# Layer 0, second token group: memory attention beside the output gate, its output parked in the recurrence's key tiles

## The chip, the cores and the metric

The kernel runs on one core of a Trainium2 chip. The metric is the device time of one execution in microseconds (us). Before the change the median of three runs is 2419.86 us (2419.42 to 2420.16).

## What is computed

One inference step of a two-layer decoder. 1024 prompt tokens (one sequence) and 8 sample tokens (one each of 8 sequences) share all weights. Layer 0's mixer, cut to what matters here:

```python
def a_mixer(hn, w_in, lb, hg_gain, mem_k, mem_v, w_o, s0):
    q_h, f_h, i_h, g_h, q_m = jnp.split(hn @ w_in, 5, axis=-1)
    ...
    o, S = hgrn2_scan(q, k, v, logf, s0)
    o = rmsnorm(o.astype(hn.dtype), hg_gain) * jax.nn.silu(g_h).reshape(B, L, HG_HEADS, HG_DV)
    om = mem_attend(q_m.reshape(B, L, MEM_HEADS, MEM_DH), mem_k, mem_v)
    out = jnp.concatenate([o.reshape(B, L, MIX_HALF), om.reshape(B, L, MIX_HALF)], axis=-1) @ w_o
    return out, S

def mem_attend(q, mk, mv):
    s = jnp.einsum('blhd,bmhd->bhlm', q.astype(jnp.float32), mk.astype(jnp.float32)) * (q.shape[-1] ** -0.5)
    p = jax.nn.softmax(s, axis=-1)
    return jnp.einsum('bhlm,bmhd->blhd', p, mv.astype(jnp.float32)).astype(q.dtype)
```

There are 4 heads of 128, and 256 memory tokens. The prompt tokens attend to one memory, projected inside the kernel; each sample token attends to a cached memory of its own and carries a recurrence state of its own, 4 heads of 128 x 128, which is read, updated and written back. A SwiGLU feed-forward network (FFN) follows each mixer; layer 1's mixer is another kind of attention.

## The kernel before

The tokens are held in two groups with features on the partitions: group 0 has 512 prompt tokens, group 1 has 512 prompt tokens and the 8 sample tokens. Every float32 product of a projection is split into a high and a low part and takes three matmuls. A projection's matmuls all come from the helper at L222, 24 of 128 x 512 or (group 1) 48 of 128 x 260 for 128 output features and 1024 input features; the weights are loaded by SyncE (L203) and split by ScalarE (L208) and VectorE (L209). Activations are split in the same way by L229 (ScalarE) and L230 (VectorE).

The code is made of Python generators. `weave` (L178) takes generators with a rate each and advances the one that has made the least progress for its rate; this sets the order in which instructions are written. A scheduler then orders them on each engine. Every engine, SyncE's transfers included, executes in that order and waits in it.

Around the change there are two weaves, called here stage A and stage B:

- **Stage A** (L1729) weaves group 1's sample recurrence (`a1.sample`), its output gate (`a1.gate`, L247 to L251: a clamp, three activations and a product), a part of group 0's FFN (`f0.part(1)`) and sums of weights on the DMA queues (`w0`).
- **Stage B** weaves first the product of gate and recurrence (`a1.merge`), then the prompt tokens' memory attention (`a1.mem`), and beside them the sample tokens' memory attention (`a1.mem_sample`) and the rest of group 0's FFN.

The prompt tokens' memory attention (`mem_attn`, L967) loads the memory's keys and values (L970, L971) into two tiles, and then goes through 8 steps, two for each head: scores (L1010), maximum (L1015), exponentials with their sums (L1021), reciprocal and scaling (L1025, L1027), transposes (L978) with a copy out of PSUM (L983) one step later, and the values (L991) two steps later. After two steps a head is complete and `put` splits it into the input tiles `xo` of the output projection (L229, L230).

The sample recurrence (`hgrn_sample`, L1222) transposes the values (L1225), writes them to DRAM (`vd`, L1229) and reads them back broadcast to all partitions. For each head it loads the state and the broadcast values (L1240, 512 KB each) one head ahead, multiplies both (L1253, L1254), adds (L1255), stores the new state (L1256), multiplies by the queries (L1257), splits the result (L229, L230) and sums it by four matmuls (L1262). After the last head the result goes through DRAM (`od`, L1270 and L1272) to be transposed (L1275).

The sample tokens' memory attention (`sample_scores`, L1037, and what follows it) writes the queries to DRAM (`qd`, L1049) and reads one broadcast per token into a tile of pool B (L1055), loads the token's keys (L1099), multiplies and reduces (L1057, L1058); the scores of all 8 tokens are then transposed (L1125).

Pools that matter: C has 4 tiles of 512 KB, for the states, the broadcast `vd`, the memory's keys and values and the cached keys and values alike. B has 7 tiles of 256 KB, T has 3 (the gate's and the FFN's intermediates), A has 8 (the recurrence's forget gates F, keys K and queries Q, two each, and the memory queries `Qm`; the gate's result `sg` takes the next that comes free). In PSUM, `S` has 3 single banks, `NS` one, and `mm` two pairs, which the projections of L222 use in turn; a pair is free when VectorE (L247, L819, L414) has read it.

Of the kernel before, what the change touches and what calls it, by code (L numbers as in the profile page):

```python
# [23 lines left out]
def tile_decoder(  # L24
# [6 lines left out]
    nc = tc.nc  # L31
# [4 lines left out]
    H = 4  # L36
# [4 lines left out]
    G = 512  # L41
# [56 lines left out]
    def NS():  # L98
        return nsp.tile([P, 512], F32, tag="ns", name=nm("ns"))
# [21 lines left out]
    def S():  # L121
        return smp.tile([P, 512], F32, tag="s", name=nm("s"))
# [51 lines left out]
    def chain(*gens):  # L174
        for g_ in gens:
            yield from g_

    def weave(*streams):  # L178

        live = [[0, n, g_] for g_, n in streams]  # L180
        while live:
            cur = min(live, key=lambda e: e[0] / e[1])
            cur[0] += 1
            try:
                next(cur[2])
            except StopIteration:
                live.remove(cur)
# [44 lines left out]
    def put(xo, i, cols, src):  # L232
        if isinstance(xo, list):
            split_to((xo[i][:, 0, cols], xo[i][:, 1, cols]), src)
            return
        t = B()[:, : cols.stop - cols.start]
        nc.scalar.copy(t, src)
        nc.sync.dma_start(xo[:, i, cols], t)
# [725 lines left out]
        yield  # L964


    def mem_attn(g, l, qm, xo):  # L967
        mkt, mv = C(), C()
        mk = mkt.rearrange("p a (h n) -> p (a h) n", n=NM)
        nc.sync.dma_start(mk, mks[l])  # L970
        nc.sync.dma_start(mv, mvs[l])  # L971
        po, asked, turned = None, None, None

        def turn(pe):
            pt = S()
            for mb in range(2):
                for j in range(2):
                    nc.tensor.transpose(  # L978
                        pt[:, (mb * 2 + j) * P : (mb * 2 + j + 1) * P],
                        pe[:, j * NM + mb * P : j * NM + (mb + 1) * P], ident,  # L980
                    )
            pts = B()
            nc.scalar.copy(pts[:, :512], pt)  # L983
            return pts

        def values(h, pr, pts):
            nonlocal po
            if pr == 0:
                po = S()
            for mb in range(2):  # L990
                nc.tensor.matmul(  # L991
                    po[:, pr * 256 : (pr + 1) * 256], mv[:, mb, h * P : (h + 1) * P],
                    pts[:, mb * 256 : (mb + 1) * 256], start=(mb == 0), stop=(mb == 1),
                )
            if pr:
                put(xo, H + h, slice(0, G), po)

        def step(new=None):
            nonlocal asked, turned
            old, turned = turned, asked and (*asked[:2], turn(asked[2]))  # L1000
            asked = new
            if old:
                values(*old)

        for h in range(H):
            for pr in range(2):
                ps = S()
                for j in range(2):
                    t0 = (2 * pr + j) * P
                    nc.tensor.matmul(  # L1010
                        ps[:, j * NM : (j + 1) * NM], qm[h // 2][:, h % 2, t0 : t0 + P], mk[:, h, :],
                        start=True, stop=True,
                    )
                nmx = small([P, 2], tag="nmx")
                nc.vector.tensor_reduce(  # L1015
                    nmx, ps.rearrange("p (j n) -> p j n", j=2), axis=AX.X, op=ALU.max, negate=True
                )
                sm = small([P, 2], tag="sme")
                pe = B()
                for j in range(2):  # L1020
                    nc.scalar.activation(  # L1021
                        pe[:, j * NM : (j + 1) * NM], ps[:, j * NM : (j + 1) * NM], AF.Exp,
                        bias=nmx[:, j : j + 1], accum_out=sm[:, j : j + 1],
                    )
                nc.vector.reciprocal(sm, sm)  # L1025
                for j in range(2):
                    nc.vector.tensor_scalar(  # L1027
                        pe[:, j * NM : (j + 1) * NM], pe[:, j * NM : (j + 1) * NM], sm[:, j : j + 1], None,
                        op0=ALU.mult,
                    )  # L1030
                step((h, pr, pe))
                yield
        for _ in range(2):
            step()
            yield
# [186 lines left out]
    def hgrn_sample(Ft, Kt, Qt, vs):  # L1222
        pvv = S()
        for h in range(H):
            nc.tensor.transpose(pvv[:NB, h * P : (h + 1) * P], vs[:, h, :], ident)  # L1225
        vT = B()
        nc.vector.tensor_copy(vT[:NB, :512], pvv[:NB, :])
        vd = tc.dram_tile([NB, 512], F32, name=nm("vd"))
        nc.sync.dma_start(vd, vT[:NB, :])  # L1229
        yield  # L1230
        HB = H * NB
        assert 2 * H == NB

        def fetch(h):
            st, vb = C(), C()
            for t, src in (
                (st, state_hgrn[0, :, h].rearrange("b k v -> k b v")),
                (vb, vd[:, h * P : (h + 1) * P].partition_broadcast(P)),
            ):
                nc.sync.dma_start(t.rearrange("p a (b v) -> p (a b) v", v=P), src)  # L1240
            return st, vb

        nxt = fetch(0)
        yield
        po = S()
        for h in range(H):
            def col(t):
                return t[h // 2][:, h % 2, G : G + NB].unsqueeze(2).to_broadcast([P, NB, P])

            st, vb = nxt  # L1250
            nxt = h < H - 1 and fetch(h + 1)
            stv, vbv = (t.rearrange("p a (b v) -> p (a b) v", v=P) for t in (st, vb))
            nc.vector.tensor_mul(stv, stv, col(Ft))  # L1253
            nc.vector.tensor_mul(vbv, vbv, col(Kt))  # L1254
            nc.vector.tensor_add(st, st, vb)  # L1255
            nc.sync.dma_start(st_sample[0, :, h].rearrange("b k v -> k b v"), stv)  # L1256
            nc.vector.tensor_mul(vbv, stv, col(Qt))  # L1257
            for a in range(2):
                qs = B(F32R), B(F32R)
                split_to(qs, vb[:, a, :])  # L1260
                for i, p in enumerate(qs):
                    nc.tensor.matmul(  # L1262
                        po[:NB, :], selr[:, 2 * h + a, :], p,
                        start=(h == 0 and a == 0 and i == 0), stop=(h == H - 1 and a == 1 and i == 1),
                    )
            yield
        rows = B()
        nc.vector.tensor_copy(rows[:NB, :], po[:NB, :])
        od = tc.dram_tile([H, NB, P], F32, name=nm("od"))
        nc.sync.dma_start(od.rearrange("h (a b) v -> (h a) b v", a=2), rows[:NB, :].rearrange("p (b v) -> p b v", v=P))  # L1270
        ot = B()
        nc.sync.dma_start(ot[:NB, :].rearrange("p (h v) -> p h v", v=P), od.rearrange("h b v -> b h v"))  # L1272
        pr = S()
        for h in range(H):
            nc.tensor.transpose(pr[:, h * NB : (h + 1) * NB], ot[:NB, h * P : (h + 1) * P], ident[:NB, :NB])  # L1275
        oc = small([P, HB], tag="ss")
        nc.scalar.copy(oc, pr[:, :HB])
        osq = small([P, HB], tag="ss")
        nc.scalar.activation(osq, oc, AF.Square)
        r = rstd_from(osq, HB, 1.0 / P, small([P, HB], tag="ss"), S)  # L1280
        for h in range(H):
            nc.vector.scalar_tensor_tensor(
                Ft[h // 2][:, h % 2, G : G + NB], oc[:, h * NB : (h + 1) * NB], hgn, r[:, h * NB : (h + 1) * NB],
                op0=ALU.mult, op1=ALU.mult,
            )
        yield
# [99 lines left out]
    class mixer_a:  # L1386
# [37 lines left out]
                yield  # L1424

        def mem(self):
            yield from mem_attn(self.g, 0, self.Qm, self.xo)

        def mem_sample(self):
            yield from mem_attn_sample(0, self.Qm, self.xo)  # L1430
# [156 lines left out]
    class mixer_b:  # L1587
# [25 lines left out]
            yield from sb_prompt(self.g, self.Qs, self.xo)  # L1613

        def mem(self):
            yield from mem_attn(self.g, 1, self.Qm, self.xo)

        def sb_sample(self):
            yield from sb_sample(self.Qs, self.xo)
# [99 lines left out]
    a1 = mixer_a(1, x1)  # L1719
    weave((chain(a0.gate(), a0.merge()), 8), (start(1, x1), 14))  # L1720
    w0 = weight_sums(0, (3, 4, 2))
# [3 lines left out]
    weave((o0.finish(), 17), (chain(a1.v(), a1.qm(A)), 8), (islice(w0, 12), 13))  # L1725
    f0 = ffn(0, 0, o0.x)
    weave((a1.core(), 22), (f0.part(0), 9), (islice(w0, 16), 17))
    a1.open()
    weave((a1.sample(), 6), (a1.gate(), 4), (f0.part(1), 9), (w0, 9))  # L1729

    def rest():
        yield from f0.part(2)
        set_banks(True)
        fw = ffn_w(0, 0, o0.x, (5, 6, 5), 3, False, f0.R)
        yield from fw.part(3)
        yield from fw.part(4)
        f0.acc = fw.acc

    weave((chain(a1.merge(), a1.mem()), 30), (a1.mem_sample(), 50), (rest(), 24))
    xk0, xb0 = [], []  # L1740
    o1 = out_proj(1, 0, M)
    drain(o1.mm(a1.xo, 0, 1, True))
# [29 lines left out]
    f0 = ffn(0, 1, o0.x)  # L1772
# [51 lines left out]
```

## Time and profile before

| | |
|---|---|
| median of 3 runs | 2419.86 us |
| the profiled execution: time, span, mean granted clock | 2420.19 us, 2418.5 us, 0.997 |
| TensorE (PE) | 99% busy |
| VectorE (DVE) | 72% busy |
| ScalarE (ACT) | 53% busy |
| GpSimd (POOL) | 5% busy |
| DMA, mean over the span | 148 GB/s |

TensorE is busy nearly always, and it executes in program order. What is read from the profile is therefore its few waits: where they are, which engine ended them, and what that engine had waited for. The views used are the busy shares of the page, the list of waits, a table of stretches of 20 us (busy time of each engine, granted clock of TensorE, DMA share), and the timeline of single engines. In the timeline a row has its start, its duration, engine, line, operation, output and inputs, the count of instructions taken together, and in brackets the idle time before it with the engine that ended it. A group's duration runs to the end of its last instruction; from start to start of two rows is what the first one cost.

### The profile page before, as it was taken

How to read it: one execution, taken by the hardware profiler on the slowest of the kernel's cores; microseconds unless marked ns; L12 is line 12 of the kernel's file. 1: busy time of each engine (PE TensorE's matmuls, PEld its weight loads, DVE VectorE, ACT ScalarE, POOL GpSimd, SP SyncE). 2: the span in 40 equal slices, each digit the busy share in tenths (PEclk: the TensorE clock that was granted, in tenths of full speed). 3: DMA queues.
4: the chain of work that ended last, by engine and by line, in shares of the span. 5: the costliest groups of instructions: out<-in, count | busy, mean ns of one | idle time of the engine just before them, and what ended most of it. 6: DMA issues, size and time to landing. Idle time of an engine off the chain costs nothing. (4 is left out here: it accounts for less than half of the span.)

```text
span 2418.5 us, 42360 instructions
## 1 busy us (share of the span) xinstructions
PE 2385.4 (99%) x15959; PEld 2158.9 (89%) x15959; DVE 1732.6 (72%) x3218; ACT 1285.2 (53%) x2560; POOL 118.5 (5%) x187
## 2 busy tenths in 40 slices
PE   8999999999999999999999999999999999999998
PEld 6888988887779998899999989877778899999998
DVE  5867557665787676878566776788788678766866
ACT  5547544354445554666544554555554457554445
POOL 1000201110000000000002200021000000000000
PEclk9999999999999999999999999999999999999999
DMA  6454666577645446432568846455353353343342
GB/s 188 123 166 117 170 189 158 133 182 191 192 132 146 152 136 207 138 101 85 148 173 232 234 138 189 153 165 148 105 165 120 97 162 122 118 129 100 107 130 76
DMA packets 510991, 357.59 MB, mean 148 GB/s; under 512 B 20109, under 2 KB 459514, under 8 KB 510786
## 3 DMA queue, kind: packets, MB, share of 16 engines
q1 hardware_dynamic: 494914, 312.93, 43.4%
q0 software_dynamic: 15872, 41.95, 7.4%
q8 instruction: 126, 2.06, 0.3%
q14 instruction: 79, 0.65, 0.1%
HBM read 322.86 MB, written 65.49 MB: 161 GB/s over the span
## 5 line engine op out<-in xcount | busy, mean ns | idle before, releaser
L222 PE MATMUL mm<-x,ws 128*128 128x512 f32 (+1 forms) x5016 | 924.5, 342 | 5.3 <-DVE t L247 2.9
L222 PEld LDWEIGHTS mm<-x,ws 128*128 128x128 f32 x5016 | 776.6, 188 | 116.9 <-issue 3.7
L208 ACT CAST ws<-w 128x512 fp32r<-128x512 f32 x596 | 347.9, 585 | 433.1 <-PE mm L222 258.9
L209 DVE TENSOR_TENSOR ws<-w,ws 128x512 fp32r<-128x512 f32 x596 | 380.8, 644 | 223.7 <-ACT ws L208 218.8
L751 PE MATMUL q<-m,ws 128*128 128x260 f32 (+1 forms) x2496 | 306.3, 283 | 1.0 <-DVE ws L209 0.4
L751 PEld LDWEIGHTS q<-m,ws 128*128 128x128 f32 x2496 | 300.3, 188 | 3.4 <-ACT m L229 0.8
L578 PE MATMUL q<-y,ws 128*128 128x260 f32 (+1 forms) x1920 | 250.9, 284 | 1.5 <-ACT q L586 1.0
L578 PEld LDWEIGHTS q<-y,ws 128*128 128x128 f32 x1920 | 238.2, 188 | 3.7 <-ACT q L586 1.4
L578 PE MATMUL q<-x,ws 128*128 128x260 f32 (+1 forms) x1668 | 218.6, 283 | 0.2 <-DVE ws L573 0.2
L578 PEld LDWEIGHTS q<-x,ws 128*128 128x128 f32 x1668 | 207.4, 188 | 0.5 <-DVE ws L573 0.4
L222 PE MATMUL mm<-m,ws 128*128 128x512 f32 x768 | 194.1, 403 | 0.2 <-DVE r L414 0.2
L571 ACT CAST ws<-w 128x512 fp32r<-128x512 f32 x206 | 124.7, 618 | 98.0 <-PE q L751 33.0
L573 DVE TENSOR_TENSOR ws<-w,ws 128x512 fp32r<-128x512 f32 x206 | 139.2, 688 | 48.9 <-ACT ws L571 45.0
L222 PEld LDWEIGHTS mm<-m,ws 128*128 128x128 f32 x768 | 143.4, 190 | 32.0 <-DVE r L414 0.7
L760 DVE TENSOR_TENSOR r<-r,q 128x260 f32<-128x260 f32 (+1 forms) x160 | 60.7, 420 | 50.9 <-PE q L751 50.6
L504 PE MATMUL q<-x,ws 128*128 128x260 f32 (+1 forms) x720 | 89.7, 283 | 0.0
L504 PEld LDWEIGHTS q<-x,ws 128*128 128x128 f32 x720 | 87.5, 188 | 0.6
L571 ACT CAST ws<-b 128x512 fp32r<-128x512 f32 x82 | 50.5, 620 | 43.6 <-PE q L751 13.8
L229 ACT CAST m<-t 128x512 fp32r<-128x512 f32 (+1 forms) x88 | 54.8, 623 | 31.0 <-DVE t L619 13.2
L573 DVE TENSOR_TENSOR ws<-b,ws 128x512 fp32r<-128x512 f32 x82 | 56.2, 688 | 18.4 <-ACT ws L571 17.8
L230 DVE TENSOR_TENSOR m<-t,m 128x512 fp32r<-128x512 f32 (+1 forms) x88 | 60.6, 689 | 11.0 <-ACT m L229 10.2
L277 DVE TENSOR_TENSOR st<-st,n 128x512 f32<-128x512 f32 (+1 forms) x91 | 62.1, 690 | 3.6 <-ACT n L276 2.5
(411 smaller groups left out, 3094.4 us busy)
## 6 DMA issues: line engine op xcount, KB each, us to landing
w<-in_w_gu SPq DMA_DIRECT2D x275, 256.0 KB, 3.3
w<-in_w_down SPq DMA_DIRECT2D x160, 256.0 KB, 2.9
wsum<-in_w_gu POOLq DMA_DIRECT2D x48, 512.0 KB, 6.0
w<-in_w_in_a SPq DMA_DIRECT2D x80, 256.0 KB, 3.0
w<-in_w_o SPq DMA_DIRECT2D x64, 256.0 KB, 2.8
w<-wsum SPq DMA_DIRECT2D x61, 256.0 KB, 3.5
b<-in_w_gu SPq DMA_DIRECT2D x39, 256.0 KB, 3.3
b<-wsum SPq DMA_DIRECT2D x39, 256.0 KB, 4.0
```

The lines of the kernel that those rows point to most:

```text
L208: nc.scalar.copy(ws[:, 0, :n, :], raw[:, :n, :])
L209: split[0] = nc.vector.tensor_sub(ws[:, 1, :n, :], raw[:, :n, :], ws[:, 0, :n, :].bitcast(F32))
L222: nc.tensor.matmul(ps[:, a, : PW[g]], wt, xt[k][:, xi, o : o + PW[g]], start=(k == 0 and wi == 0), stop=(k == nk - 1 and wi == 2),)
L229: nc.scalar.copy(dst[0], src)
L230: nc.vector.tensor_sub(dst[1], src, dst[0].bitcast(F32))
L277: nc.vector.tensor_add(acc[:, :n], acc[:, :n], t[:, :n])
L504: ins = nc.tensor.matmul(pp[a][:, :h], wt, xt[k][:, xi, a * h : (a + 1) * h], start=(k == 0 and wi == 0), stop=(k == ND - 1 and wi == 2),)
L571: nc.scalar.copy(w[:, 0, :], src)
L573: split[0] = nc.vector.tensor_sub(w[:, 1, :], src, w[:, 0, :].bitcast(F32))
L578: nc.tensor.matmul(ps[:, :h], w[:, wj, k * P : (k + 1) * P], x[:, xi, :], start=(first and k == 0 and wi == 0), stop=(k == 3 and wi == 2), ...
L751: nc.tensor.matmul(pp[a][:, :h], wt, mids[k][:, xi, a * h : (a + 1) * h], start=(k == 0 and wi == 0), stop=(k == nf - 1 and wi == 2),)
L760: nc.vector.tensor_add(d, d, pp[a][:, :h])
```

## The change

The memory attention of group 1's prompt tokens is woven into stage A, beside the sample recurrence and the gate. At that point the tiles of `xo` are not yet to be had: they are opened behind stage A now. So each completed head is copied by ScalarE into a half of one of the recurrence's key tiles K (512 columns of it; the sample tokens' 8 columns, which the recurrence still reads, are left alone). In stage B, `a1.unpark` splits the parked heads into `xo` behind `a1.merge`. The accumulator of the sample recurrence moves from an `S` bank to the `NS` bank. The rates of the two weaves change.

```diff
-    def mem_attn(g, l, qm, xo):
+    def mem_attn(g, l, qm, out):
...
             if pr:
-                put(xo, H + h, slice(0, G), po)
+                out(h, po)
...
         nxt = fetch(0)
         yield
-        po = S()
+        po = NS()
...
         def mem(self):
-            yield from mem_attn(self.g, 0, self.Qm, self.xo)
+            yield from mem_attn(self.g, 0, self.Qm, lambda h, po: put(self.xo, H + h, slice(0, G), po))
+
+        def parked(self, h):
+            return self.K[h // 2][:, h % 2, :G]
+
+        def mem_parked(self):
+            yield from mem_attn(self.g, 0, self.Qm, lambda h, po: nc.scalar.copy(self.parked(h), po))
+
+        def unpark(self):
+            for h in range(H):
+                put(self.xo, H + h, slice(0, G), self.parked(h))
+                yield
...
+    weave((a1.sample(), 6), (a1.gate(), 4), (a1.mem_parked(), 11), (f0.part(1), 9), (w0, 9))
     a1.open()
-    weave((a1.sample(), 6), (a1.gate(), 4), (f0.part(1), 9), (w0, 9))
...
-    weave((chain(a1.merge(), a1.mem()), 30), (a1.mem_sample(), 50), (rest(), 24))
+    weave((chain(a1.merge(), a1.unpark()), 20), (a1.mem_sample(), 50), (rest(), 24))
```

Group 0 and layer 1 use `mem_attn` as before, with `put` handed in.

Three places in the order of the instructions. The first is SyncE in stage A, before: the second half of head 0 and head 1 of the recurrence. `c` are the C tiles, `w` weights.

```order
L1240 DMA c_5442<-vd_5205 128x8x128
L1240 DMA c_5595<-in_state_hgrn 128x8x128
L203 DMA w_5450<-in_w_gu 128x4x128
L1240 DMA c_5596<-vd_5205 128x8x128
L203 DMA w_5487<-in_w_gu 128x4x128
L1256 DMA out_st_sample<-c_5441 128x8x128
L203 DMA w_5492<-in_w_gu 128x4x128
L1240 DMA c_5784<-in_state_hgrn 128x8x128
```

And after the change, from head 1's broadcast to head 2's:

```order
L1240 DMA c_5667<-vd_5197 128x8x128
L203 DMA w_6008<-in_w_down 128x4x128
L203 DMA w_6013<-in_w_down 128x128
L1256 DMA out_st_sample<-c_5666 128x8x128
L203 DMA w_6035<-in_w_down 128x4x128
L203 DMA w_6040<-in_w_down 128x128
L1240 DMA c_5899<-in_state_hgrn 128x8x128
L203 DMA w_6108<-in_w_down 128x4x128
L203 DMA w_6113<-in_w_down 128x128
L203 DMA w_6135<-in_w_down 128x4x128
L1240 DMA c_5900<-vd_5197 128x8x128
```

Before, head 1's state and broadcast (`c_5595`, `c_5596`) are issued ahead of head 0's store; now head 1's store comes first, then head 2's state into the tile that was stored, and head 2's broadcast into the tile that head 1's splits have read. Weights stand between and behind.

The second place is VectorE in stage A. Before, between head 0's and head 1's products (`mm` are PSUM pairs, `t` tiles of pool T, `a_5207` the gate's result, `ws` weights):

```order
L1257 TENSOR_TENSOR c_5442<-c_5441,a_2692 128x1024
L1254 TENSOR_TENSOR c_5596<-c_5596,a_2294 128x1024
L251 TENSOR_TENSOR t_5309<-t_5309,t_5308 128x512
L209 TENSOR_TENSOR ws_5406<-w_5404,ws_5406 128x512
L819 TENSOR_TENSOR t_5309<-t_5309,mm_5325 128x512
L230 TENSOR_TENSOR b_5605<-c_5442,b_5604 128x512
```

After, from head 1's products to head 2's, with a step of memory attention between them (`nmx`, `sme` and `b_5777` are its maximum, its sums and its probabilities; `a_5199` the gate's result):

```order
L1257 TENSOR_TENSOR c_5667<-c_5666,a_2692 128x1024
L209 TENSOR_TENSOR ws_5923<-w_5921,ws_5923 128x512
L1015 TENSOR_REDUCE nmx_5774<-s_5771 128x2
L251 TENSOR_TENSOR a_5199<-a_5199,t_5259 128x520
L251 TENSOR_TENSOR a_5199<-a_5199,t_5637 128x520
L1253 TENSOR_TENSOR c_5899<-c_5899,a_2494 128x1024
L1025 RECIPROCAL sme_5776<-sme_5776 128x2
L1027 TENSOR_SCALAR b_5777<-b_5777,sme_5776 128x256 x2
L251 TENSOR_TENSOR t_5723<-t_5723,t_5722 128x512
L209 TENSOR_TENSOR ws_5928<-w_5926,ws_5928 128x512
L819 TENSOR_TENSOR t_5723<-t_5723,mm_5739 128x512
```

Head 2's state (`c_5899`) now has to be there before the attention's scaling and before the FFN's L819, which frees the pair `mm_5739`. TensorE transposes `b_5777` directly ahead of the projection `mm_5845`, which takes that pair next. On TensorE the projections stand in the same sequence as before, with the attention's steps between them.

The third place is SyncE in stage B, where the query broadcasts of the 8 sample tokens are issued. Before, six of them (`b_6327` to `b_6528`) stand ahead of the memory's keys and values, and the last two here, behind the third pair of keys and nine more weights:

```order
L203 DMA w_7018<-in_w_gu 128x4x128
L1055 DMA b_6631<-qd_6242 128x512
L1055 DMA b_6637<-qd_6242 128x512
L1099 DMA c_6736<-in_cache_mem_v 128x2x512
L1099 DMA c_6782<-in_cache_mem_v 128x2x512
```

After, all eight stand together:

```order
L203 DMA w_6655<-in_w_gu 128x4x128
L1055 DMA b_6507<-qd_6422 128x512
L1055 DMA b_6513<-qd_6422 128x512
L1055 DMA b_6603<-qd_6422 128x512
L1055 DMA b_6609<-qd_6422 128x512
L203 DMA w_6660<-in_w_gu 128x4x128
L1055 DMA b_6699<-qd_6422 128x512
L1055 DMA b_6705<-qd_6422 128x512
L1055 DMA b_6792<-qd_6422 128x512
L1055 DMA b_6801<-qd_6422 128x512
L1099 DMA c_6697<-in_cache_mem_k 128x2x512
```

What moved: the two broadcasts that stood behind the memory attention's tiles in pool B come ahead of the third pair of keys.

More of the change, by code (lines that the diff above doesn't have):

```diff
@@ L1615, in mem @@
         def mem(self):
-            yield from mem_attn(self.g, 1, self.Qm, self.xo)
+            yield from mem_attn(self.g, 1, self.Qm, lambda h, po: put(self.xo, H + h, slice(0, G), po))
         def sb_sample(self):
```

## Prediction

> **What bounds the kernel now.** I read the page's busy shares first, then the waits of TensorE, then the table by stretches of 20 us, and last the timeline around each wait that the change can touch. The page:
>
> ```profile
> PE 2385.4 (99%) x15959; PEld 2158.9 (89%) x15959; DVE 1732.6 (72%) x3218; ACT 1285.2 (53%) x2560; POOL 118.5 (5%) x187
> ```
>
> TensorE has 33 us of the 2418.5-us span in which it isn't busy, so nothing can be won but its waits, and time in which it runs at a lower clock. TensorE executes in program order; what the change moves costs it the same in the new place. Its waits, in us in total, times, longest:
>
> ```profile
> PE mm L222 <- DVE t L247: 2.9, 1, 2.9
> PE s L1125 <- DVE sc L1058: 2.9, 1, 2.9
> PE mm L222 <- DVE ws L209: 1.2, 2, 0.8
> ```
>
> The first falls in the stretch with the output gate (stage A, from 506 to 622 us), the second in the one with the mem attention (stage B, from 622 us on). The columns of the stretches: width and busy TensorE, then the other engines, PEclk as granted clock, DMA share and GB/s.
>
> ```profile
> 520.00:540.00 20.00, 20.00 (x88) 16.26 (x87) 19.98 (x27) 12.33 (x22) 2.42 (x3) 1.00 0.81 222
> 560.00:580.00 20.00, 19.35 (x78) 15.22 (x78) 11.86 (x20) 11.55 (x21) 1.47 (x2) 0.91 0.69 182
> 660.00:680.00 20.00, 16.98 (x74) 13.21 (x74) 14.33 (x25) 8.65 (x19) 0.00 (x0) 0.95 0.55 159
> 680.00:700.00 20.00, 20.00 (x83) 15.39 (x82) 16.18 (x30) 8.28 (x20) 0.00 (x0) 0.88 0.44 138
> ```
>
> Behind each of the two long waits the granted clock is below 1.00, so a wait costs more than its length. How much, the timeline of TensorE in stage A says (start, duration, and in brackets the idle time before):
>
> ```profile
> 552.09 5.71 PE L222 MATMUL mm<-x,ws 128*128 128x512 f32 x24
> 560.65 18.46 PE L222 MATMUL mm<-x,ws 128*128 128x512 f32 x72 [2.85 <-DVE t L247]
> 578.95 1.09 PE L1262 MATMUL s<-b,selr 128*8 128x512 f32 x4
> 579.88 5.91 PE L222 MATMUL mm<-x,ws 128*128 128x260 f32 x48
> ```
>
> A block of 24 matmuls of 512 columns takes 5.57 us from start to start at full clock (5.71 with the last one's end). 72 of them are 16.7 us; here they took 578.95 - 560.65 = 18.3. **The stall costs 2.85 + 1.6 = 4.4 us.** In stage B:
>
> ```profile
> 678.70 0.59 PE L1125 MATMUL s<-ident,sc 128*32 128x128 f32 x2 [2.85 <-DVE sc L1058]
> 679.46 5.49 PE L222 MATMUL mm<-m,ws 128*128 128x512 f32 x12 [0.17 <-DVE r L414]
> 684.87 0.34 PE L1135 MATMUL s<-ident,b 32*128 32x32 f32 x2
> ```
>
> Twelve matmuls, 2.8 us by the same rate, took 5.4: **2.85 + 0.17 + 2.6 = 5.6 us.**
>
> **The change, part by part.** *Removed from stage B.* The second wait comes from these rows:
>
> ```profile
> 657.17 10.91 PE L222 MATMUL mm<-x,ws 128*128 128x512 f32 x46 [0.48 <-DVE ws L209]
> 669.91 0.97 SPq L1055 DMA_DIRECT2D b<-qd x2
> 673.93 2.36 DVE L1057 TENSOR_TENSOR c<-c,b 128x1024 f32<-128x1024 f32 x2 [1.03 <-DMA b<-qd]
> 676.21 2.34 DVE L1058 TENSOR_REDUCE sc<-c 128x8 f32<-128x1024 f32 x2
> ```
>
> The last two query broadcasts are issued at 669.9, because mem attention holds tiles of the B pool; VectorE's four operations behind them (4.6 us) end just before L1125 starts. With the attention gone from stage B, the order of the changed kernel has all eight broadcasts issued together, and L1125 at the same place among the FFN's matmuls. The 5.6 us go, and the 0.48 of the L209 wait at 657 in the same crowded stretch: **-6.1 us**. What is late next is the key loads and VectorE's L1057/L1058, covered by the seven blocks of 24 matmuls, 39 us, that stand between L1045 and L1125 in both. I book 0 for it, with 1.5 us as the other end.
>
> *Added work.* Four copies to the parking tiles on ScalarE; the counts of matmuls and VectorE operations are the same. Price by the nearest row, the L983 copy of the same shape:
>
> ```profile
> L983 ACT COPY b<-s 128x512 f32<-128x512 f32 x32 | 18.7, 585 | 2.5 <-PE s L978 2.4
> L1015 DVE TENSOR_REDUCE nmx<-s 128x2 f32<-128x512 f32 x32 | 21.8, 683 | 0.1
> L1021 ACT ACTIVATE b<-s,nmx 128x256 f32<-128x256 f32 x64 | 29.8, 470 | 13.4 <-DVE nmx L1015 11.4 <-DMA c<-in_cache_mem_v 1.8
> L1021 ACT ACTIVATION_READ_ACCUMULATOR b<-s,nmx 128x1 f32 x64 | 12.6, 197 | 0.0
> L1027 DVE TENSOR_SCALAR b<-b,sme 128x256 f32<-128x256 f32 x64 | 19.8, 348 | 0.4
> ```
>
> 4 x 0.585 = 2.3 us on an engine that is 53% busy: 0 on the path, unless one stands before a split that TensorE waits for (below). A whole step of mem attention costs TensorE, in stage B at full clock:
>
> ```profile
> 707.67 1.02 PE L1010 MATMUL s<-c,a 128*128 128x256 f32 x4
> 708.53 0.60 PE L978 MATMUL s<-ident,b 128*128 128x128 f32 x4
> 708.97 1.03 PE L991 MATMUL s<-b,c 128*128 128x256 f32 x4
> 709.64 0.58 PE L1069 MATMUL ns<-n,selr 128*8 128x512 f32 x1
> ```
>
> 709.64 - 707.67 = 1.97 us (L1010 0.86, L978 0.44, L991 0.67). These are paid in stage A instead: net 0.
>
> *Moved: the C tiles.* This is the step that costs. The mem keys and values now hold two of the four C tiles all through stage A, where the recurrence's sample loop had all four: a state and a `vd` broadcast for this head, and the same for the next. In the new order, head h+1's state load stands behind head h's store of the same tile, and its `vd` load behind head h's last split. I measure that chain by the old one. SyncE, then VectorE:
>
> ```profile
> 520.90 0.38 SPq L1256 DMA_DIRECT2D out_st_sample<-c  x1
> 524.88 0.37 SPq L1240 DMA_DIRECT2D c<-in_state_hgrn  x1
> 532.17 1.86 SPq L1256 DMA_DIRECT2D out_st_sample<-c  x1
> 539.71 0.37 SPq L1240 DMA_DIRECT2D c<-in_state_hgrn  x1
> 547.78 0.37 SPq L1240 DMA_DIRECT2D c<-vd  x1
> ```
>
> ```profile
> 544.35 1.21 DVE L1253 TENSOR_TENSOR c<-c,a 128x1024 f32<-128x1024 f32 x1
> 555.20 1.23 DVE L1254 TENSOR_TENSOR c<-c,a 128x1024 f32<-128x1024 f32 x1 [6.84 <-DMA c<-vd]
> 559.82 0.68 DVE L247 TENSOR_SCALAR t<-mm 128x520 f32<-128x520 f32 x1
> ```
>
> Each of these two state loads takes the tile of the store ahead of it: **4.0 us** (524.88 - 520.90) or 7.5 from the store's issue to the load's. The load issued at 539.71 was in use at 544.35: at most **4.6**. The `vd` load issued at 547.78 let VectorE go on at 555.20: 7.4. The medians of the page for loads of this size:
>
> ```profile
> c<-vd SPq DMA_DIRECT2D x4, 512.0 KB, 7.2
> c<-in_cache_mem_v SPq DMA_DIRECT2D x16, 512.0 KB, 3.7
> ```
>
> A lone `vd` load is not in the trace; it lies between 3.7 and 7.4, and I take 6.6, a bit under its own median, because fewer large transfers now run beside it. The last two rows also show the first wait: VectorE stood 6.84 us for the fourth `vd`, L247 behind it freed a PSUM pair only at 560.5, TensorE waited 2.85. In the new order L247 no longer follows such a load: **-4.4 us**.
>
> Now the new places, on a clock that starts with the first gate block at 506.3 as before and adds 5.57 per 24 matmuls, 5.86 per 48 of 260 columns, 0.93 per four L1262, and the mem steps:
>
> 1. Head 0's splits stand behind the fourth score step. Scores end at 556.5; the maximum (0.68), two exponentials (1.34), two copies (1.2) and two casts (1.2) end at 560.9 and VectorE's second split at 561.5. TensorE reaches L1262 at 560.1 and spreads the four over 1 us: **0.5** lost.
> 2. `vd` of head 1 is issued at 561.5 and lands at 568.1; two operations of 1.2 until the store, 570.5; state 2 issued 4.0 later, usable 4.6 later: 579.1. L1253 (1.2), reciprocal and L1027 (0.5): 580.8. TensorE comes to the L978 that transposes this result after two blocks of 48, nine of 24, 8.9 us of mem steps, one L1262 group and the 0.5 lost: 506.3 + 11.7 + 50.1 + 8.9 + 0.9 + 0.5 = 578.4: **2.4**. Behind it VectorE does L1027, L251, a weight's L209 and L819 (2.2) before mm_5739's PSUM pair is free for mm_5845, at 583.0; TensorE, with 0.44 of work, waits **1.7** more.
> 3. Head 1's last split comes ten VectorE operations later, near 588.8: `vd` 595.4, store 597.8, state 3 usable at 606.4, L1253 and L414 at 608.2. TensorE's mm_6118, which needs the PSUM pair that this L414 frees, is due at 606.9 (583.0 + 5.6 + 0.7 + 0.9 + 5.9 + 2.0, then 30 matmuls of 512 at 7.0 and a step of 1.9): **1.3**.
> 4. `vd` of head 3 takes the keys' tile, so it waits for the last L1010, at 605.8: it lands at 612.4, and VectorE's L1254 and the split of head 2 behind it end at 614.2. TensorE's L1262 inside mm_6118 is due 2.55 after 608.2, at 610.8: **3.4**.
>
> That is 9.3 us. One of these gaps is longer than 2.85, which halved the clock twice here: 2.1, the mean of 1.6 and 2.6. **Stage A: +11.4 - 4.4 = +7.0.**
>
> The clock rule of the Trainium skill, "TensorE: Matmul & The Clock Gate", section "What's actually happening", says that the array falls to half clock after an idle window of about 3.4 us, counted by a free-running window. The two rows with 2.85 us of idle time disagree on the length: the clock fell after less. By the page's rule the gain would be only the waits themselves, 2.85 + 2.85 + 0.65, against 9.3 + 2.1, near +5 us; by the rows it is 10.5 against 11.4. I go by the rows.
>
> **Sum:** -6.1 + 7.0 = +0.9 on the profiled execution, 2420.19 us (its span and 1.7 around it), which lies 0.3 above the median 2419.86 of the three runs. On the median: **2420.8, I say 2421**. What can be told from no change here is 0.2%, 4.8 us: faster is below 2415.0, slower above 2424.7.
>
> Bounds. With `vd` at 3.7, waits 2 to 4 shrink to 1.1 + 0 + 1.9, with 0.5 of the first and no halved clock 3.5: -7.0, 2413. With each store at 7.5 and `vd` at 7.4, waits 2 and 3 become 8.3 and 5.6, wait 4 is hidden in 3: 14.4 with the first, and three halved clocks of 2.1: +10.2, 2430.
>
> **The rivals.**
> - *Faster, near 2413.* The loads land early because half as many 512-KB transfers overlap; the first bound. For it: the DMA share of 0.81 in the stretch where the slow ones ran, and the 3.7 of the mem_v loads. Against it: weights still stream beside them, and `vd` is read back as a broadcast. Chance 0.23.
> - *Slower, near 2430.* The hand-over of one C tile, store then load, sits on TensorE's path at the L978 of mm_5845 and at mm_6118, with the store at 7.5 as at 532.17. It decides from a store landing of about 6 us: then waits 2 and 3 are 6.0 and 3.3, wait 4 is 1.4, the first stays 0.5, and with two halved clocks 15.4 us stand against 10.5. For it: one of the two measured hand-overs took 7.5. Against it: the other took 4.0, and fewer large transfers will run beside these. Chance 0.24.
> - *The stall in stage B doesn't go, near 2427.* If L1057 is late for the keys instead of the queries, stage A's +7.0 stands alone. For it: the order still has key loads in one C rotation. Against it: only 1.03 us of wait there names a DMA, and it names the queries. Chance 0.08.
>
> "Double-buffer for performance" among the Best Practices of the Trainium skill, "Trainium Kernel Development and Optimization", speaks against this change, since the loop over the heads loses its second pair of tiles; its result would be the slower rival's 2430. The old rows agree only in part: with two pairs VectorE still stood 6.84 us for a `vd`.
>
> **How the numbers follow.** My case has 0.45. The range of 8 in 10 runs from the fast bound to the slow one, 2413 to 2431. Faster by over 0.2%: 0.23, nearly all from the first rival. Slower: 0.24 and 0.08 make 0.32. Same: 0.45.
>
> **What would show it.** Right: no L1125 wait, and PEclk 1.00 from 660 to 700; no wait of mm on L247 near 557; VectorE waits for `c<-vd` and `c<-in_state_hgrn` at L1253 and L1254, with TensorE waits for L1027, L819, L414 and L230 between 575 and 620, some 9 us in all. Wrong: if those waits sum to under 4 us or over 15, the lengths of the loads were wrong; if they name ScalarE, it is the exponentials and parking copies that I priced at 0.5; if L1125 still waits, stage B was misread.

## The result, and the profile after

| | before | after |
|---|---|---|
| median of 7 runs | 2418.93 us (2417.05 to 2420.16) | 2426.58 us (2425.45 to 2429.98) |
| profiled execution, its span | 2420.19, 2418.5 us | 2425.89, 2424.2 us |

The changed kernel takes 1.0036 times the time of before, with a 95% interval of 1.0026 to 1.0046; the medians lie 7.6 us apart. The profiled executions lie 5.7 us apart, since the one of before is the longest of its seven, and these 5.7 are what is taken apart below. TensorE's waits after the change, as in the list of waits of before (us in total, times, longest):

```profile
PE s L978 <- DVE b L1027: 2.4, 3, 2.0
PE ns L1262 <- DVE b L230: 2.3, 1, 2.3
PE ns L1262 <- ACT b L229: 2.0, 1, 2.0
...
PE mm L222 <- DVE t L819: 1.3, 1, 1.3
```

The two waits of 2.9 us of before are not in the list any more; four others are. The longest entry of both lists is left out, here and in the prediction: 9.7 us before and 9.6 after at L363, which the change doesn't touch. TensorE's timeline places the four (in brackets the idle time), and shows L1125 without a wait:

```profile
506.18 0.60 PE L1225 MATMUL s<-ident,vs 128*8 128x128 f32 x4
580.77 0.72 PE L978 MATMUL s<-ident,b 128*128 128x128 f32 x4 [2.04 <-DVE b L1027]
582.75 7.39 PE L222 MATMUL mm<-x,ws 128*128 128x512 f32 x24 [1.25 <-DVE t L819]
613.42 0.40 PE L1262 MATMUL ns<-b,selr 128*8 128x512 f32 x1 [1.97 <-ACT b L229]
618.37 1.02 PE L1262 MATMUL ns<-b,selr 128*8 128x512 f32 x2 [2.31 <-DVE b L230]
648.37 0.41 PE L1275 MATMUL s<-ident,b 8*128 8x8 f32 x4 [0.70 <-DMA b<-od]
699.52 0.39 PE L1125 MATMUL s<-ident,sc 128*32 128x128 f32 x2
757.54 1.59 PE L578 MATMUL q<-x,ws 128*128 128x256 f32 x12
```

The same landmarks in the timeline of before:

```profile
505.97 0.60 PE L1225 MATMUL s<-ident,vs 128*8 128x128 f32 x4
621.65 0.41 PE L1275 MATMUL s<-ident,b 8*128 8x8 f32 x4 [0.52 <-DMA b<-od]
752.75 1.77 PE L578 MATMUL q<-x,ws 128*128 128x256 f32 x12
```

From L1225 to L1275 (stage A) TensorE took 115.7 us before and takes 142.2 now. The moved attention is 15.8 of that (8 steps of 1.97), so stage A is 10.7 us worse. From L1275 to L578 (stage B) it was 131.1 and is 109.2: with 15.8 moved away, 6.1 us better. That is +4.6 of the 5.7; the other 1.1 lie outside, 0.2 ahead and 0.9 behind. In the table by stretches (PEclk is the column of 0.91), the stage's lost clock:

```profile
580.00:600.00 20.00, 17.97 (x98) 15.31 (x99) 15.48 (x28) 7.69 (x17) 2.24 (x4) 0.91 0.62 150
600.00:620.00 20.00, 15.72 (x64) 11.79 (x63) 10.03 (x20) 7.59 (x19) 1.32 (x2) 0.85 0.59 127
620.00:640.00 20.00, 20.00 (x105) 16.84 (x104) 11.42 (x20) 8.91 (x18) 1.26 (x3) 0.89 0.73 218
660.00:680.00 20.00, 20.00 (x88) 16.15 (x87) 19.82 (x24) 10.60 (x19) 0.00 (x0) 1.00 0.78 243
680.00:700.00 20.00, 20.00 (x89) 16.14 (x89) 19.21 (x29) 7.88 (x14) 0.00 (x0) 1.00 0.75 224
```

Stage B now has a clock of 1.00 where before it had 0.95 and 0.88. Stage A loses 0.09, 0.15 and 0.11 of three times 20 us: 7.0 us of full speed. The waits are 7.6 us in four places and 0.2 more at L1275. Less the 4.4 us of the stall that went, that makes 10.4, against 10.7 measured; up to 1.2 us of the lost clock lie inside the last wait and are counted twice, so the sum is between 9.2 and 10.4.

What the four wait for, SyncE shows first:

```profile
561.77 0.37 SPq L1240 DMA_DIRECT2D c<-vd  x1
570.08 0.38 SPq L1256 DMA_DIRECT2D out_st_sample<-c  x1
574.93 0.37 SPq L1240 DMA_DIRECT2D c<-in_state_hgrn  x1
588.97 0.37 SPq L1240 DMA_DIRECT2D c<-vd  x1
597.20 0.38 SPq L1256 DMA_DIRECT2D out_st_sample<-c  x1
602.19 0.37 SPq L1240 DMA_DIRECT2D c<-in_state_hgrn  x1
609.73 0.50 SPq L1240 DMA_DIRECT2D c<-vd  x1
```

and then VectorE, which stands at each of these loads:

```profile
567.57 1.23 DVE L1254 TENSOR_TENSOR c<-c,a 128x1024 f32<-128x1024 f32 x1 [1.53 <-DMA c<-vd]
578.94 1.23 DVE L1253 TENSOR_TENSOR c<-c,a 128x1024 f32<-128x1024 f32 x1 [3.02 <-DMA c<-in_state_hgrn]
594.61 1.23 DVE L1254 TENSOR_TENSOR c<-c,a 128x1024 f32<-128x1024 f32 x1 [1.75 <-DMA c<-vd]
606.40 1.23 DVE L1253 TENSOR_TENSOR c<-c,a 128x1024 f32<-128x1024 f32 x1 [3.16 <-DMA c<-in_state_hgrn]
610.15 0.68 DVE L1015 TENSOR_REDUCE nmx<-s 128x2 f32<-128x512 f32 x1
616.49 1.23 DVE L1254 TENSOR_TENSOR c<-c,a 128x1024 f32<-128x1024 f32 x1 [3.75 <-DMA c<-vd]
```

Read in order of time, it is one chain: `vd` 561.8 to 567.6, the store at 570.1, the state 574.9 to 578.9, TensorE at 580.8; `vd` 589.0 to 594.6, the store, the state 602.2 to 606.4; then VectorE comes late to the attention's maximum (610.15), and ScalarE behind it to the cast of head 2:

```profile
610.87 0.47 ACT L1021 ACTIVATE b<-s,nmx 128x256 f32<-128x256 f32 x1 [3.42 <-DVE nmx L1015]
612.72 0.64 ACT L229 CAST b<-c 128x512 fp32r<-128x512 f32 x1
```

So the wait that the list puts down to ScalarE begins with a state load too, two engines earlier. The attention is a link of it: the products that the cast of head 2 reads were ready at 598.4, and the cast came at 612.72 because the attention's exponentials and copies stand ahead of it on ScalarE, and those behind the late maximum.

### The profile page after: what moved, and what is told of

Its sections match the earlier page's. It is cut to its first block, busy times and chain, and to the rows that moved or that the text cites. A ratio compares the mean times of both kernels' runs of the same rounds, so it can differ in the third digit from the quotient of the medians.

```text
span 2424.2 us, 42333 instructions
## 1 busy us (share of the span) xinstructions
PE 2387.5 (98%) x15959; PEld 2160.4 (89%) x15959; DVE 1735.0 (72%) x3218; ACT 1284.2 (53%) x2562; POOL 114.8 (5%) x187
## 3 DMA queue, kind: packets, MB, share of 16 engines
q8 instruction: 126, 2.06, 0.4%
## 5 line engine op out<-in xcount | busy, mean ns | idle before, releaser
L578 PE MATMUL q<-y,ws 128*128 128x260 f32 (+1 forms) x1920 | 250.7, 284 | 1.0 <-ACT q L586 0.5
L578 PEld LDWEIGHTS q<-y,ws 128*128 128x128 f32 x1920 | 238.2, 189 | 3.0 <-ACT q L590 0.9
L578 PE MATMUL q<-x,ws 128*128 128x260 f32 (+1 forms) x1668 | 218.4, 283 | 0.2 <-DVE ws L573 0.2
L578 PEld LDWEIGHTS q<-x,ws 128*128 128x128 f32 x1668 | 207.3, 189 | 0.5 <-DVE ws L573 0.4
L230 DVE TENSOR_TENSOR m<-t,m 128x512 fp32r<-128x512 f32 (+1 forms) x88 | 60.7, 690 | 11.5 <-ACT m L229 10.9
```

Of the source, the lines that this page charges most:

```text
L230: nc.vector.tensor_sub(dst[1], src, dst[0].bitcast(F32))
L578: nc.tensor.matmul(ps[:, :h], w[:, wj, k * P : (k + 1) * P], x[:, xi, :], start=(first and k == 0 and wi == 0), stop=(k == 3 and wi == 2), ...
```

## The experiments

**Theory:** TensorE waits for the loads of the recurrence, which come later because the attention holds two C tiles, through VectorE's queue. **Rival:** the attention's own work on ScalarE and VectorE stands ahead of the splits and evacuations. Ratios are to the kernel before on the same chip, which measured 2415 to 2416 us there (17 to 27 runs), with 95% intervals.

**The changed kernel again.** No edit.

> The changed kernel once more, beside the next two on one chip, since the kernel before measures 2416 there and 2419 where it was profiled. Theory: its waits stand at the same four places (L978 of the sixth score step, the projection behind it, the L1262 of head 2), with lengths that follow the loads; the ratio to before is 1.003 to 1.004 again, 2423 to 2426 us. Rival (the time differs by where the two ran, not by the kernel): a ratio within 0.001 of 1.

2426.12 us, ratio 1.0048 (1.0034 to 1.0062). Waits at the same places of 1.7, 1.25, 0.55 and 3.29 us. The loss is the kernel's, a little above the 1.003 to 1.004 expected. That its size follows the loads is not shown.

**No loads for heads 1 to 3.**

```diff
+        first = []
...
         def fetch(h):
+            if first:
+                return first
             st, vb = C(), C()
+            first[:] = [st, vb]
...
-            nc.sync.dma_start(st_sample[0, :, h]...
+            if h == H - 1:
+                nc.sync.dma_start(st_sample[0, :, h]...
```

> The changed kernel with the states and vd loaded for head 0 alone and the other heads computing in the same two tiles; only the last head is stored (three heads' states, their loads and their stores are left out, the arithmetic is the same in number). Theory (TensorE waits for loads and for the stores ahead of them, through VectorE's queue): all four waits of the changed kernel in stage A go, no half clock there, 10 to 13 us below the changed kernel, 4 to 6 below before. Rival (the attention's exponentials, copies and scalings delay the splits and the evacuations): the waits for L229 at L1262 stay at 2 us or more, and less than 6 us are won.

2415.24 us, ratio 1.0001 (0.9992 to 1.0010): 10.9 us below the changed kernel. The stretches of stage A, same columns:

```profile
560.00:580.00 20.00, 20.00 (x90) 15.78 (x89) 15.60 (x23) 12.49 (x26) 1.54 (x2) 1.00 0.22 53
580.00:600.00 20.00, 19.98 (x116) 17.18 (x115) 14.63 (x25) 8.31 (x21) 0.77 (x2) 1.00 0.40 106
600.00:620.00 20.00, 20.00 (x115) 16.89 (x115) 14.71 (x24) 10.79 (x23) 2.45 (x4) 1.00 0.75 196
```

TensorE is busy throughout at full clock, with all of the attention's and the recurrence's arithmetic in place. That decides against the rival as a cause by itself: without late loads, the attention's work delays nothing. The second half of the expectation, 4 to 6 us below before, failed, for a reason that the next run shows in part.

**The NS bank alone.** Before, with `po = NS()` in place of `po = S()`.

> The kernel before with one part of the change alone: the accumulator of the sample recurrence in the NS bank in place of an S bank. Theory (the loss is the C tiles and the queues behind them): nothing, within 1 us of before; its trace also shows stages A and B of the old order on the same chip as the other runs. Rival (the single NS bank makes something wait): 1.5 us or more above before, with a wait at L1262 or at the next user of NS.

2414.72 us, ratio 0.9997 (0.9988 to 1.0006): nothing. Its trace shows the old order where the experiments ran:

```profile
PE s L1125 <- DVE sc L1058: 2.4, 1, 2.4
...
PE mm L222 <- DVE t L247: 1.0, 1, 1.0
```

The wait behind the fourth `vd` is 1.0 us here, with no half clock behind it, and 2.85 in the first trace of before. The same order of instructions had less to lose here, so less could be won. From L1225 to L578, stages A and B together, this trace takes 240.8 us and the one without loads 238.4; outside both stages the latter takes 2.5 us more, and why stays open.

**The keys and values out of the C tiles.** Each head's 256 columns of keys and 256 of values in one tile of pool B:

```diff
-        mkt, mv = C(), C()
...
-        nc.sync.dma_start(mk, mks[l])
-        nc.sync.dma_start(mv, mvs[l])
...
+                t = B()
+                nc.sync.dma_start(t[:, :NM], mks[l][:, h, :])
+                nc.sync.dma_start(t[:, NM:]..., mvs[l][:, :, h * P : (h + 1) * P])
...
```

> The changed kernel, but the parked attention loads keys and values head by head into one tile of pool B each (256 columns of keys, 256 of values), so the recurrence has all four C tiles again. Theory (the loss is the C tiles: store, state load and vd load of one head after the other, 7.6 us of TensorE waits, and the half clock behind them, some 5 us): VectorE no longer waits 3 us for states at L1253, the waits of TensorE for L1027, L819, L229 and L230 between 575 and 620 us shrink to under 2 us, PEclk is 1.00 there, and the gain of stage B stays: 2411 to 2415 us, below the kernel before (2419). Rival (the attention's own work on ScalarE and VectorE stands ahead of the splits and the FFN's evacuations): the same places wait as long as now, 2424 to 2428.

2422.23 us, ratio 1.0026 (1.0017 to 1.0035). The waits fell from four to two, 1.7 us for L819 and this one:

```profile
PE ns L1280 <- ACT b L229: 3.4, 1, 3.4
```

The expectation failed: four C tiles give back part, not all. VectorE still stands for loads in front of the work that TensorE needs:

```profile
544.38 1.22 DVE L1272 TENSOR_TENSOR c<-c,a 128x1024 f32<-128x1024 f32 x1 [4.68 <-DMA c<-vd]
557.95 1.23 DVE L1271 TENSOR_TENSOR c<-c,a 128x1024 f32<-128x1024 f32 x1 [2.56 <-DMA c<-in_state_hgrn]
```

The wait of 3.4 us again ends with a cast that stands behind the attention's exponentials on ScalarE, as the rival says; those wait for a maximum that VectorE reaches only after the state.

**No stores for heads 0 to 2.** The store under `if h == H - 1`, the loads kept.

> The changed kernel without the stores of the new state of heads 0 to 2 (those rows of one output are left out), so a state load no longer waits until a store has landed. Theory: the state loads start 4 to 5 us earlier, the waits at L978 (2.0) and mm after it (1.25) go with the 3.4 us of half clock behind them; the two L1262 waits of head 2 (4.3 us with 10 us at half clock) stay, since the fourth vd still waits for the keys' tile: 2420 to 2423 us. Rival (ScalarE's and VectorE's work): no change beyond 1 us, 2425.5 to 2427.5.

2421.01 us, ratio 1.0017 (1.0008 to 1.0026). By the ratios that is 5 to 7 us below the changed kernel's two measurements. The wait at L978 went, as expected, but of the one behind it, which was to go too, 1.1 us stayed. At the L1262 of head 2 one wait of 4.3 us stood: the fourth state could still be loaded only when VectorE had read the tile for head 2 (L1257 in the changed kernel), at 603.

**The attention earlier.** Rate 24 for `mem_parked` in place of 11.

> The changed kernel with the attention at rate 24 in place of 11 in stage A: it ends by the middle of the stage, so head 2's state and everything behind it have four C tiles again. Theory: the wait for the last L1010 by the fourth vd goes, and the L1262 waits of head 2 (4.3 us and 10 us of half clock) with it; a wait in the denser first half may be new: 3 to 6 us below the changed kernel. Rival (the attention's work on VectorE and ScalarE is what delays): the denser attention makes the first half worse by as much, no gain or up to 5 us above.

2422.37 us, ratio 1.0029 (1.0018 to 1.0041), 3.8 us below the changed kernel and within the 3 to 6 expected. The L1262 waits fell to 0.9 us, but a new one of 4.3 us stands in the first half, where two steps of attention are queued behind head 1's state:

```profile
529.28 1.23 DVE L1253 TENSOR_TENSOR c<-c,a 128x1024 f32<-128x1024 f32 x1 [1.64 <-DMA c<-in_state_hgrn]
```

**First the recurrence, then the attention.**

```diff
-    weave((a1.sample(), 6), (a1.gate(), 4), (a1.mem_parked(), 11), ...
+    weave((chain(a1.sample(), a1.mem_parked()), 17), (a1.gate(), 4), ...
```

> The changed kernel with the recurrence's sample loop and the parked attention in a chain in stage A (first the one, then the other, rate 17) in place of side by side. Theory: the recurrence has four C tiles, the attention takes two when it is done. The waits of the changed kernel in stage A go; a wait for a vd load of up to 3 us with its half clock (the one of before) may come back; stage B as in the changed kernel: 2412 to 2417 us. Rival (parking and the attention in stage A cost in themselves, by B, T and S tiles): 2421 or more.

2420.34 us, ratio 1.0012 (1.0003 to 1.0022), above the 2412 to 2417 expected and short of the rival's 2421. One long wait is left in stage A, 3.9 us at the last L1262 of head 1. It stands behind a `vd` for which VectorE waited 1.69 us: the recurrence now ran too fast for its own loads. The same with an empty step behind each of the recurrence's:

```diff
+    weave((chain(padded(a1.sample(), 1), a1.mem_parked()), 22), (a1.gate(), 4), ...
```

> As the run with the sample loop first and the attention behind it, but with each step of the sample loop followed by an empty one (rate 22), so that the splits of head 1 aren't asked for directly behind those of head 0. Theory (in that run only the 3.9-us wait of L1262 for a late vd stood in the way): that wait and its half clock (1.7) go, 3 to 6 us below before. Rival (the attention has too little cover at the end of stage A, with 4 to 15 matmuls between its steps): waits of 3 us and more at L978, L991 or L1010, between before and 5 us above it.

2412.76 us (11 runs), ratio 0.9988 (0.9979 to 0.9997). **This version beats the changed kernel by far.** Against before it is 3.1 us faster, at the lower end of the expectation, with an interval that stops just short of none; by the 0.2% of the prediction that is no change yet, and the run with the NS bank alone lay 1.2 us below before without having won anything. The attention's matmuls wait 0.2 us at most, so the rival's waits didn't come. Its stretches from 560 us:

```profile
560.00:580.00 20.00, 20.00 (x100) 15.90 (x99) 11.66 (x19) 9.36 (x16) 2.88 (x4) 1.00 0.77 210
580.00:600.00 20.00, 19.77 (x105) 16.54 (x104) 12.49 (x30) 8.50 (x22) 1.19 (x3) 1.00 0.54 129
600.00:620.00 20.00, 19.78 (x119) 17.47 (x117) 14.25 (x30) 12.35 (x31) 2.19 (x4) 1.00 0.37 108
```

The loads are all in place here, and so is all of the attention's work; only their order differs. With the run without loads this says that the loss takes both: late loads, and the attention's work queued between them.

**Stage B alone.** Two kernels that are the one before but for a rate in stage B: 15 in place of 30 for merge and attention, or 70 in place of 50 for the sample tokens' attention.

> The kernel before with only the rate of merge and attention in stage B lowered from 30 to 15, so that the attention's first scores come behind the sample tokens' L1125 and all eight query broadcasts are issued together; nothing is moved to stage A and nothing is parked. Theory (what stage B won was the order of the query broadcasts, not the absence of the attention): the L1125 wait of 2.85 us and its half clock go, 5.6 to 6.1 us: 2413 to 2414 us, if the attention finds cover later; up to 2417 if its last steps become late. Rival (stage B was short of VectorE and ScalarE, so the attention must leave it): the stall comes back in another place, 2418 to 2421.

> The kernel before with the sample tokens' attention at rate 70 in place of 50 in stage B, so that its eight query broadcasts come first and L1125 two blocks earlier, with the prompt tokens' attention beside FFN matmuls behind it. Theory (stage B can be had without moving the attention, if it keeps cover): no L1125 wait, 3 to 6 us below before. Rival (without the attention's VectorE and ScalarE work out of the way, stage B stalls elsewhere, as it did with the attention at half its rate): 3 us or more above before.

2429.26 us, ratio 1.0051 (1.0037 to 1.0065), and 2423.34 us, ratio 1.0032 (1.0019 to 1.0044). Neither has the L1125 wait. The first has its attention among layer 0's last FFN products, where ScalarE stands 3.78 us for weights and takes 1.28 us to load an activation table ahead of the exponentials:

```profile
748.43 2.08 PE L1010 MATMUL s<-c,a 128*128 128x256 f32 x4 [5.39 <-ACT b L1021]
```

In the second, TensorE waits 1.5 us twice near 645 us and 1.6, 1.0 and 1.0 at L1069 near 705. The theory failed in both: by these rates stage B couldn't be relieved without moving the attention out.

**No attention.** `mem_parked` left out of stage A.

> The changed kernel with group 1's memory attention of layer 0 left out (the heads that are put into the output projection's input are the keys of the recurrence); stage A is otherwise that of before, stage B that of after. TensorE has 8 x 1.97 = 15.8 us less to do. Theory (stage B without the attention wins 6 to 7 us, and stage A with four C tiles costs what it did before): 22 to 23 us below before. Rival (stage B's win is taken back later, VectorE being full): 15 to 18 us below before. The distance from the changed kernel to this one, less 15.8, is what the attention in stage A costs beyond its own matmuls: by the theory 14 to 15 us.

2396.90 us, ratio 0.9919 (0.9905 to 0.9933): 19.0 below before, between the two expectations. 15.8 are the attention's matmuls; stage B's win here is less than 6.1, since the L1125 wait it removes was 2.4 us in the trace with the NS bank alone, not 2.85 with a longer half clock. From that trace to this one, L1275 to L578 goes from 128.9 us to 109.4: 3.6 won beside the 15.8. The distance to the changed kernel's second measurement is 29 us by the medians and 31 by the ratios; less 15.8 that is 13 to 15, against the 14 to 15 expected, and the interval of each ratio reaches 0.14%, 3.4 us, to either side.

## Why the prediction was right or wrong

The time, 2426.6, lay in the range of 2413 to 2431, on the slower side; the forecast itself was 2421, within 0.2% of before, and the kernel came out slower by 0.36%, which had 0.32. The forecast change was +0.9 us and the measured one +7.6: that the time lay inside owes much to the width of the range.

- **Stage B, -6.1:** -6.1 in the trace. The broadcasts issued together removed the L1125 wait, and nothing came late in its place. Where the old wait was shorter (2.4), the win was too: 3.6 us in the trace without attention.
- **The old stall behind the fourth `vd`, -4.4:** gone.
- **The copies, 0:** nothing waits for them alone, and with the loads gone (but the copies still there) no wait is left. One does stand directly ahead of the cast that ends the 1.97-us wait, and so has 0.5 us of it (612.24 to 612.72).
- **The C tiles:** the loads took 5.8, 5.6 and 6.8 us for `vd` (6.6 assumed), 4.9 and 5.0 for the store until the next load (4.0), 4.0 and 4.2 for the state (4.6). State 3 was usable at 606.4, as worked out, which is luck: the `vd` ahead of it came 1 us faster than assumed, and the next load after the store 1 us later.
- **The places:** wait 2 was put at 2.4 and 1.7 and came out at 2.04 and 1.25. Wait 1 (0.5) was none. Wait 3 (1.3 at mm_6118) was none either, since TensorE itself came 1.6 us later to it, at 608.55 and not 606.9; what the late state did instead was to delay the exponentials ahead of head 2's cast, 1.97. Wait 4 (3.4) was 2.31. Together 7.6 us against 9.3.
- **The step that failed** is "One of these gaps is longer than 2.85, which halved the clock twice here: 2.1". No gap was longer than 2.31, and yet the clock was halved from 583.33 to 586.74 and from 614.05 to 624.29, which is 6.8 us of full speed (5.7 without what lies in the last wait). I had taken the length of a single gap as what counts. The rows show otherwise (width, busy TensorE, the other engines, PEclk, DMA share, GB/s):

```profile
576.50:579.91 3.41, 2.23 (x10) 1.53 (x9) 0.97 (x1) 2.57 (x6) 0.00 (x0) 1.00 0.48 145
579.91:583.33 3.42, 1.30 (x7) 0.94 (x8) 3.38 (x9) 0.55 (x2) 0.00 (x0) 1.00 0.01 3
583.33:586.74 3.41, 3.41 (x10) 2.67 (x9) 2.84 (x7) 3.38 (x10) 1.07 (x2) 0.50 0.53 95
610.63:614.05 3.42, 1.45 (x7) 0.89 (x6) 0.98 (x4) 2.50 (x7) 0.45 (x1) 1.00 1.03 192
614.05:617.46 3.41, 2.01 (x5) 1.02 (x4) 0.97 (x1) 1.75 (x3) 0.00 (x0) 0.50 0.93 159
617.46:620.87 3.41, 2.50 (x6) 1.55 (x7) 3.41 (x7) 0.00 (x0) 0.00 (x0) 0.50 0.38 52
620.87:624.29 3.42, 3.42 (x9) 2.63 (x8) 0.98 (x1) 0.13 (x1) 0.00 (x0) 0.50 1.01 324
```

  The first spell has two gaps before it, 2.04 and 1.25 with 0.7 us of work between, of which 2.1 us lie in the 3.4 us ahead of the fall. The second has one: the clock fell at 614.05, 0.6 us after the gap of 1.97 and 2.0 us before the gap of 2.31 began; that one lies at half clock, and the clock stayed halved until 624.29. This term was 3.6 to 4.7 us too small; less the 1.7 by which the waits were too large, that is half or more of the miss of stage A (+10.7 against +7.0). The rest stays open.
- **The rivals:** the slower one had the time nearly right (2430) but not for its reason: stores at 7.5 us weren't seen, nor the 6 from which it would decide; its two halved clocks (4.2 us) were nearer to the 5.7 to 6.8 measured than my one. The faster one's loads of 3.7 us for `vd` weren't seen either. In the third, L1125 would still wait; it doesn't.

On the clock the page of the Trainium skill, "TensorE: Matmul & The Clock Gate", section "What's actually happening", has a window of about 3.4 us that is free-running. The prediction set it aside because 2.85 us had been enough. Part of it would have served: the spells at half clock are whole multiples of 3.41 us, one and three of them here, and they begin on a grid of that width that runs on from one to the other (614.05 - 583.33 is nine times 3.413). What the trace doesn't bear out is the whole idle window that the page asks for: 1.97 and 2.1 us of idle time in one stretch were enough.

What stays open is how the loss divides between the two C tiles and the queue: freeing the tiles gave back 2 to 5 us (by the ratios to before), taking the loads away 10.9.

## What to carry to other kernels

Work that shares an in-order engine with a loop that loads and stores inherits the loop's waits: here the attention's maximum and scaling, and the FFN's evacuations, stood in VectorE's queue behind a state load. Put such work behind the loop, and count tiles before interleaving: two held tiles turned a prefetch into a chain of store, load, compute. Price small stalls by the idle time that falls together into a few microseconds, with the clock that this costs, and not one by one.

## What the runs showed of the hardware

The granted clock changes on a grid. In all 13 traces, between the first 20 us and the last 10, every fall and every rise lies a multiple of 3.413 us behind the clock's first rise. By these traces, idle time of TensorE inside one stretch of that grid decides. All 16 stretches at full clock with 1.96 us or more of it had half clock behind them; none with less than 1.5 had; of three between (1.55, 1.69 and 1.76) the first two had. Half clock ended behind a stretch with 0.54 us or less and went on behind one with 0.71 or more.

So the length of a gap alone says little. The grid cuts the single gap of 2.06 us in the run without attention into 0.82 and 1.24, and the clock stays at 1.00:

```profile
555.06:558.47 3.41, 2.59 (x12) 1.76 (x10) 3.41 (x5) 0.00 (x0) 0.00 (x0) 1.00 0.64 126
558.47:561.88 3.41, 2.17 (x10) 1.80 (x11) 2.99 (x5) 2.28 (x5) 0.00 (x0) 1.00 0.87 230
```

The two gaps of 1.55 and 1.54 us in the run with rate 70 put 2.00 us into one stretch, and the clock halves. Nor does the length of the spell follow the gap: 4.28 us (no stores) and 2.4 (the NS bank alone) were both followed by 3.41 us at half clock, 3.36 (keys and values in pool B) by 6.83, since that gap reaches 1.37 us into the first stretch at half clock.

How soon a load lands varies enough to matter: the wait of TensorE behind the fourth `vd` in the old order of stage A was 2.85 us in the trace of before, 1.02 with the NS bank alone, 1.9 in both runs on stage B alone and 2.06 without attention. It varies between runs on one chip, so it can't be put down to the chip.
